# State scan of an S5 mixer on VectorE: products reordered, sums done in two halves

## The chip, the cores and the metric

One core of one Trainium2 chip. The metric is the device time of one execution of the whole program in microseconds (us); the median of the runs stands for a kernel. The engines are called PE (TensorE, the matrix engine), DVE (VectorE), ACT (ScalarE), POOL (GpSimd) and SP (SyncE, which issues transfers).

## The reference

An encoder of two layers over 1040 tokens (16 learned ones in front of 1024) of width 1024, all in float32. Layer 0 has a bidirectional S5 state-space mixer, layer 1 grouped-query attention, and each of them is followed by a SwiGLU channel mixer. What matters here is the recurrence of the S5 mixer, in both directions:

```
def _s5_combine(left, right):
    ...
    br = ar2 * br1 - ai2 * bi1 + br2
    bi = ar2 * bi1 + ai2 * br1 + bi2
...
    _, _, sr, si = lax.associative_scan(_s5_combine, (a_r, a_i, bu_r, bu_i), reverse=reverse, axis=1)
    return (jnp.einsum('blgp,gcp->blgc', sr, c_re) - jnp.einsum('blgp,gcp->blgc', si, c_im))
```

There are 64 groups of 16 channels, and each group has 64 complex states for each direction. A state is multiplied by a complex constant (abr, abi) and the input of the step is added to it.

## The kernel before

The S5 mixer takes 8 tokens as one step (T = 8), so that 1040 tokens make 130 steps (NK). Matrix products first form the inputs of all steps, then a scan carries the state from step to step, and then matrix products read the outputs from the states (L533). The scan is a loop over i from 2 to 129 in `s5_phase`, 128 steps one after the other, since each needs the state of the one before. Both directions lie on the partitions together: 64 partitions hold the states of the forward direction, 64 those of the backward one. On the free side a state has its real and its imaginary part for 64 groups, [2, 64], 128 elements.

One step is four instructions on DVE, L507 to L510:

```
V.tensor_tensor(out=TA, in0=SB[:, 0], in1=st, op=ALU.mult)
V.tensor_tensor(out=TB, in0=SB[:, 1], in1=st, op=ALU.mult)
V.tensor_tensor(out=TS, in0=TA, in1=bi, op=ALU.add)
V.tensor_tensor(out=nx, in0=TS, in1=TB[:, ::-1], op=ALU.add)
```

`st` and `nx` are the states of step i - 1 and i in the table XS (SBUF), which held the step's input in the same place before. `bi` is that input, copied ahead. The constants SB[:, 0] (real part, twice) and SB[:, 1] (imaginary part, once with its sign turned) and the product TB are three quarters of one PSUM tile, SBT, of 2 KB in each partition; the profile calls all three SB. TA and TS lie in SBUF. `TB[:, ::-1]` swaps real and imaginary part.

The order on each engine is that of the program text; nothing moves instructions. Semaphore waits are set by the framework from the tiles that instructions read and write, also between instructions of the same engine.

The loop also gives out other work by step number. `inputs` copies the inputs of four steps at a time to PSUM, on ACT, four steps ahead (L485, tile IN, two buffers). `e_batch` builds the matrices for the read-out on POOL (L379 to L383), and `inside` makes what the tokens of a step give to each other, with products on PE (L435, L457), copies on ACT and transfers. From the middle of the scan on, `swap` turns the order of the backward states, on ACT (L469, L472, L473); its last piece comes after the last step, and then the read-out starts (L533, 256 matrix products).

After the S5 mixer's core come its two linear layers, the channel mixer, attention, and the second channel mixer, which the change doesn't touch.

Of the kernel before, what the change touches and what calls it, by code (L numbers as in the profile page):

```python
# [13 lines left out]
ALU = mybir.AluOpType  # L14
# [5 lines left out]
G = 64  # L20
# [92 lines left out]
def s5_phase(nc, tc, P, a, ident, acc, xres, ydram, late):  # L113

    V, A, PE, PO = nc.vector, nc.scalar, nc.tensor, nc.gpsimd
# [256 lines left out]
    def e_batch(gb):  # L372

        gs = slice(NB * gb, NB * gb + NB)
        g0 = NB * gb % (G // 2)
        q_r, q_s, q_d = (bc(q[:, :, gs].rearrange("p s g -> p g s"), 3, CH) for q in E3)
        c_r, c_i, c_s = (bc(c[:, gs], 2, T) for c in (Cr, Ci, Cs))
        er, ei = (Eh[2 * gb // NG][:, i, g0:g0 + NB] for i in range(2))
        PO.tensor_tensor(out=ek, in0=c_s, in1=q_r, op=ALU.mult)  # L379
        PO.tensor_tensor(out=er, in0=c_i, in1=q_s, op=ALU.mult)  # L380
        PO.tensor_tensor(out=er, in0=ek, in1=er, op=ALU.subtract)
        PO.tensor_tensor(out=ei, in0=c_r, in1=q_d, op=ALU.mult)
        PO.tensor_tensor(out=ei, in0=ei, in1=ek, op=ALU.subtract)  # L383
# [27 lines left out]
    SB, TB = SBT[:, :2], SBT[:, 2]  # L411
# [8 lines left out]
    TA = rp.tile([128, 2, G], FP32, name="TA")  # L420
    TS = rp.tile([128, 2, G], FP32, name="TS")
# [42 lines left out]
    def swap(lo, hi):  # L464

        n = hi - lo
        t = psw.tile([128, 4, 2, G], FP32, tag="t", name="t")[64:, :n]
        m0, m1 = NK - hi, NK - lo
        A.copy(out=t, in_=XS[64:, lo:hi])  # L469
        yield  # L470
        for cs, cp in [(slice(0, 2), A.copy)] if lo else [(slice(0, 1), A.copy), (slice(1, 2), V.tensor_copy)]:
            cp(out=XS[64:, lo:hi, cs], in_=XS[64:, m1 - 1:m0 - 1 if m0 else None:-1, cs])  # L472
            cp(out=XS[64:, m0:m1, cs], in_=t[:, ::-1, cs])  # L473
# [3 lines left out]
    sw = [(lo, hi) for hi, lo in zip(cuts, cuts[1:])]  # L477
    begun = []
    IN = {}

    def inputs(i):

        n = min(4, NK - i)
        t = psc.tile([128, 4, 2, G], FP32, tag="in", name="IN", bufs=2)
        A.copy(out=t[:, :n], in_=XS[:, i:i + n])  # L485
        for k in range(n):
            IN[i + k] = t[:, k]

    inputs(2)
    for i in range(2, NK):  # L490
        for gb in range(NG):
            if i == 2 + int(E_PACE * gb):
                e_batch(gb)
            l0 = L_AT + int(L_PACE * gb)
            if i == l0:
                work[gb] = [inside(gb), l0]
        for gb in list(work):
            if i >= work[gb][1]:
                at = next(work[gb][0], None)
                if at is None:  # L500
                    del work[gb]
                else:
                    work[gb][1] = L_AT + int(L_PACE * gb) + at
        if i % 4 == 2 and i + 4 < NK:
            inputs(i + 4)
        st, nx, bi = XS[:, i - 1], XS[:, i], IN.pop(i)
        V.tensor_tensor(out=TA, in0=SB[:, 0], in1=st, op=ALU.mult)  # L507
        V.tensor_tensor(out=TB, in0=SB[:, 1], in1=st, op=ALU.mult)  # L508
        V.tensor_tensor(out=TS, in0=TA, in1=bi, op=ALU.add)  # L509
        V.tensor_tensor(out=nx, in0=TS, in1=TB[:, ::-1], op=ALU.add)  # L510
        if sw and not begun and i > NK // 2:
            begun.append((sw[0][0], swap(*sw.pop(0))))
            next(begun[-1][1])
        if begun and NK - 1 - begun[0][0] <= i - 1:
            next(begun.pop(0)[1], None)
# [11 lines left out]
    for ft in range(KT):  # L527
        for g0 in range(8 * ft, 8 * ft + 8, 2):
            b = bank()
            for j in range(2):  # L530
                g = g0 + j
                for c2 in range(2):
# [3 lines left out]
                            in1=b[:, :2 * NK].rearrange("p (g k) -> p g k", g=2), op=ALU.add)  # L536
# [694 lines left out]
def whole(nc, tc, a, out):  # L1231
# [45 lines left out]
    def late():  # L1277
# [3 lines left out]
        return w.split  # L1281

    s5_phase(nc, tc, P, a, ident, acc, xdram, ydram, late)
    con = P("const2")
    N.blk = con.tile([128, 128], FP32, name="blk")
# [303 lines left out]
```

## Time and profile before

| What | Value |
|---|---|
| Median of 3 runs | 2845.06 us (2843.23 to 2846.6) |
| The profiled execution's own time | 2844.93 us |
| Its span in the trace | 2843.2 us |
| PE busy | 2649.4 us, 93% |
| DVE busy | 1559.1 us, 55%, 3025 instructions |
| ACT busy | 1154.3 us, 41% |
| POOL busy | 515.3 us, 18% |
| Mean granted clock of PE | 0.967 of full speed |

The span goes from the first to the last instruction; the execution's own time has 1.7 us around it. The busy times overlap. A line such as L507 is the line of the kernel before; "out<-in" are tiles by the program's names.

### The profile page before, as it was taken

The numbers are of one execution on the slowest core, as the hardware profiler recorded it, in microseconds if no ns is written. First come the engines' busy times: TensorE is split into PE (matmuls) and PEld (weight loads), VectorE is DVE, ScalarE is ACT, GpSimd is POOL, SyncE is SP. The second block draws the span as 40 slices with busy tenths as digits, with TensorE's granted clock in tenths as the row PEclk, the third lists the DMA queues.
The fourth block names the chain that finished last, engine by engine and source line by source line (L and its number), as shares of the span: only waits on it lengthen the run. The fifth ranks groups of instructions, "written<-read, shape, count | busy, mean of one in ns | idle before, by whom it ended". The sixth has DMA issues, their size and how long they took to land.

```text
span 2843.2 us, 43155 instructions
## 1 busy us (share of the span) xinstructions
PE 2649.4 (93%) x17277; PEld 2546.5 (90%) x17277; DVE 1559.1 (55%) x3025; ACT 1154.3 (41%) x2138; POOL 515.3 (18%) x533
## 2 busy tenths in 40 slices
PE   7657899999999999989999998999999999999997
PEld 6446899999999999988988887888999999999996
DVE  9994545733333333358768888885563333333334
ACT  7463534322212212245557778774522222222225
POOL 0770332300000000043034434431310000000002
PEclk9778999999999999999999999999999999999998
DMA  6113652221111111112111111102111111111101
GB/s 150 24 38 102 230 175 72 77 80 45 47 51 45 45 52 45 45 45 87 48 24 39 27 24 49 28 19 98 45 38 46 52 45 45 45 45 45 45 31 60
DMA packets 124836, 167.41 MB, mean 59 GB/s; under 512 B 13499, under 2 KB 104971, under 8 KB 124635
## 3 DMA queue, kind: packets, MB, share of 16 engines
q1 hardware_dynamic: 118203, 141.22, 17.5%
q0 software_dynamic: 5712, 21.30, 2.2%
q8 instruction: 136, 2.23, 0.3%
q10 hardware_dynamic: 720, 2.13, 0.2%
q14 instruction: 65, 0.53, 0.1%
HBM read 126.41 MB, written 21.23 MB: 52 GB/s over the span
## 4 chain that ended last, share of the span: by engine, by line
PE 78%; DVE 13%; ACT 4%; issue 3%; DMA 2%; POOL 1%; SPq 0%; ACTq 0%; DVEq 0%; POOLq 0%
PE bk L694 22%; PE bk L695 22%; PE bk L696 22%; PE pv L1106 4%; PE pt L1084 3%; DVE mx L1064 3%; DVE pl L1097 2%; PE b L533 2%; ACT ph L1092 1%; DVE TA L507 1%; DVE SB L508 1%; DVE XS L510 1%; PE bx L347 1%; PE b L124 1%; DVE TS L509 1%
## 5 line engine op out<-in xcount | busy, mean ns | idle before, releaser
L694 PE MATMUL bk<-Hh,unit 128*128 128x348 f32 (+1 forms) x2928 | 956.4, 327 | 9.4 <-ACT Hh L784 5.8
L695 PE MATMUL bk<-Hl,unit 128*128 128x348 f32 (+1 forms) x2928 | 945.3, 323 | 1.1 <-DVE Hl L788 1.0
L696 PE MATMUL bk<-Hh,unit 128*128 128x348 f32 (+1 forms) x2928 | 943.8, 322 | 0.0
L694 PEld LDWEIGHTS bk<-Hh,unit 128*128 128x128 f32 x2928 | 555.2, 190 | 14.7 <-ACT Hh L784 5.4
L695 PEld LDWEIGHTS bk<-Hl,unit 128*128 128x128 f32 x2928 | 554.9, 190 | 6.4 <-DVE Hl L788 2.0
L696 PEld LDWEIGHTS bk<-Hh,unit 128*128 128x128 f32 x2928 | 554.7, 189 | 0.0
L858 DVE TENSOR_TENSOR sg<-sg,bk 128x348 f32<-128x348 f32 x132 | 68.1, 516 | 632.3 <-PE bk L696 624.5
L723 POOL TENSOR_TENSOR lns<-lns,lnsq 128x348 f32<-128x348 f32 (+1 forms) x72 | 70.0, 983 | 1550.5 <-ACT lnsq L721 1549.4
L694 PE MATMUL bk<-gt,unit 128*128 128x348 f32 (+1 forms) x1056 | 340.5, 322 | 0.0
L696 PE MATMUL bk<-gt,unit 128*128 128x348 f32 (+1 forms) x1056 | 339.1, 321 | 0.0
L695 PE MATMUL bk<-gt,unit 128*128 128x348 f32 (+1 forms) x1056 | 338.5, 321 | 0.0
L881 DVE TENSOR_TENSOR acc<-acc,bk 128x348 f32<-128x348 f32 (+1 forms) x480 | 237.5, 513 | 112.7 <-PE bk L696 112.7
L860 ACT CAST gt<-sg 128x348 fp32r<-128x348 f32 x132 | 63.7, 482 | 487.6 <-DVE sg L858 487.6
L1084 PE MATMUL pt<-ident,P 128*116 128x128 f32 (+1 forms) x1188 | 181.3, 279 | 44.1 <-DVE pl L1097 39.4
L1097 DVE TENSOR_TENSOR pl<-pt,ph 116x512 fp32r<-116x512 f32 (+3 forms) x340 | 204.4, 619 | 15.0 <-ACT ph L1092 13.4
L1084 PEld LDWEIGHTS pt<-ident,P 128*116 128x116 f32 (+1 forms) x1188 | 132.5, 136 | 80.4 <-issue 30.6
L1072 POOL TENSOR_SCALAR P<-P,l 128x1044 f32<-128x1044 f32 x132 | 149.8, 1146 | 291.0 <-PE pv L1106 174.4
L694 PEld LDWEIGHTS bk<-gt,unit 128*128 128x128 f32 x1056 | 199.0, 188 | 0.5 <-issue 0.2
L695 PEld LDWEIGHTS bk<-gt,unit 128*128 128x128 f32 x1056 | 198.9, 188 | 0.5 <-issue 0.2
L696 PEld LDWEIGHTS bk<-gt,unit 128*128 128x128 f32 x1056 | 198.7, 188 | 0.0
L1092 ACT CAST ph<-pt 116x512 fp32r<-116x512 f32 (+3 forms) x340 | 168.6, 535 | 73.9 <-PE pt L1084 59.7
L609 ACT CAST unit<-raw 128x1024 fp32r<-128x1024 f32 x110 | 113.2, 1046 | 209.7 <-DMA raw<-in_ffn_w_up_dram 173.1
(287 smaller groups left out, 3928.1 us busy)
## 6 DMA issues: line engine op xcount, KB each, us to landing
raw<-in_ffn_w_gate_dram SPq DMA_DIRECT2D x44, 512.0 KB
raw<-in_ffn_w_up_dram SPq DMA_DIRECT2D x44, 512.0 KB
raw<-in_ffn_w_down_dram SPq DMA_DIRECT2D x44, 512.0 KB
y<-xdram SPq DMA_DIRECT2D x16, 520.0 KB
QA<-QH SPq DMA_DIRECT2D x30, 260.0 KB
raw<-in_attn_w_qkv_dram SPq DMA_DIRECT2D x14, 512.0 KB
xdram<-acc SPq DMA_DIRECT2D x32, 130.0 KB
xres<-xn POOLq DMA_DIRECT2D x8, 520.0 KB, 5.1
```

Of the source, the lines that this page charges most:

```text
L609: A.copy(out=u[:, 0], in_=r)
L694: mm(out, wh, xh, start=(first and i == 0), stop=False)
L695: mm(out, wh, xl, start=False, stop=False)
L696: mm(out, wl, xh, start=False, stop=(last and i == n - 1))
L723: (nc.vector if on_dve else nc.gpsimd).tensor_tensor(out=part, in0=part, in1=sq, op=ALU.add)
L881: V.tensor_tensor(out=x, in0=x, in1=b, op=ALU.add)
L1064: V.tensor_reduce(out=k.mx, in_=k.S[:, :, :348], axis=mybir.AxisListType.XY, op=ALU.max, negate=True)
L1072: PO.tensor_scalar(out=k.P, in0=k.P, scalar1=k.l, scalar2=1.0, op0=ALU.mult, op1=ALU.mult)
L1084: PE.transpose(b[:m, w * i + 128 * x:w * i + 128 * x + 128], u.P[x][:, KB_N * kt:KB_N * kt + m], self.ident)
L1092: A.copy(out=u.ph[s][:m, :w], in_=u.t[s][:m, :w])
L1097: V.tensor_tensor(out=u.pl[s][:m, :w], in0=u.t[s][:m, :w], in1=u.ph[s][:m, :w].bitcast(FP32), op=ALU.subtract)
L1106: PE.matmul(u.o[:, :u.w], VAs[u.j][:m, kt], (u.ph, u.pl)[x][s][:m, c:c + u.w], start=(kt == 0 and x == 0), stop=(kt == KBS - 1 and x == 1))
```

## The change

In a step the product TB comes first, then TA. The sum TS and the sum nx are each done in two instructions, one for groups 0 to 31 and one for groups 32 to 63, so that a step has six instructions, and the 128 steps have 768 in place of 512. What is computed is the same, element by element. Lines behind L479 stand one lower in the changed kernel's text, those behind the step three lower; there TB is L508, TA L509, TS L511 and nx L513.

```diff
     IN = {}
+    halves = [slice(0, G // 2), slice(G // 2, G)]
...
         st, nx, bi = XS[:, i - 1], XS[:, i], IN.pop(i)
+        V.tensor_tensor(out=TB, in0=SB[:, 1], in1=st, op=ALU.mult)
         V.tensor_tensor(out=TA, in0=SB[:, 0], in1=st, op=ALU.mult)
-        V.tensor_tensor(out=TB, in0=SB[:, 1], in1=st, op=ALU.mult)
-        V.tensor_tensor(out=TS, in0=TA, in1=bi, op=ALU.add)
-        V.tensor_tensor(out=nx, in0=TS, in1=TB[:, ::-1], op=ALU.add)
+        for gs in halves:
+            V.tensor_tensor(out=TS[:, :, gs], in0=TA[:, :, gs], in1=bi[:, :, gs], op=ALU.add)
+        for gs in halves:
+            V.tensor_tensor(out=nx[:, :, gs], in0=TS[:, :, gs], in1=TB[:, ::-1, gs], op=ALU.add)
```

DVE before, in the scan, from the second product of one step to the first sum of the next, in which a new block of inputs begins. SB as an output is TB, SB as an input holds the constants or TB; behind each stand the semaphores that it waits for, DVE_49 for earlier instructions of DVE itself, Activation_49 for ACT:

```order
L508 TENSOR_TENSOR SB<-SB,XS 128x128 [waits DVE_49]
L509 TENSOR_TENSOR TS<-TA,IN 128x128
L510 TENSOR_TENSOR XS<-TS,SB 128x128 [waits DVE_49]
L507 TENSOR_TENSOR TA<-SB,XS 128x128 [waits DVE_49]
L508 TENSOR_TENSOR SB<-SB,XS 128x128 [waits DVE_49]
L509 TENSOR_TENSOR TS<-TA,IN 128x128 [waits Activation_49]
```

The first sum, L509, waits for no instruction of DVE; in one step of four it waits for the copy of the inputs.

DVE in the changed kernel, the same place, from the second product, now TA, to the sums of the next step:

```order
L509 TENSOR_TENSOR TA<-SB,XS 128x128 [waits DVE_49]
L511 TENSOR_TENSOR TS<-TA,IN 128x2x32 [waits DVE_49]
L511 TENSOR_TENSOR TS<-TA,IN 128x2x32
L513 TENSOR_TENSOR XS<-TS,SB 128x2x32 [waits DVE_49] x2
L508 TENSOR_TENSOR SB<-SB,XS 128x128 [waits DVE_49]
L509 TENSOR_TENSOR TA<-SB,XS 128x128 [waits DVE_49]
L511 TENSOR_TENSOR TS<-TA,IN 128x2x32 [waits DVE_49,Activation_49]
```

The first half of TS now follows TA directly and waits for DVE, in one step of four for ACT too; its second half waits for nothing, and each half of nx has a wait of its own.

## Rows read from the trace of the kernel before

**Rows 1.** The page, chain that ended last: shares by engine and by line.
```profile
PE 78%; DVE 13%; ACT 4%; issue 3%; DMA 2%; POOL 1%; SPq 0%; ACTq 0%; DVEq 0%; POOLq 0%
PE bk L694 22%; PE bk L695 22%; PE bk L696 22%; PE pv L1106 4%; PE pt L1084 3%; DVE mx L1064 3%; DVE pl L1097 2%; PE b L533 2%; ACT ph L1092 1%; DVE TA L507 1%; DVE SB L508 1%; DVE XS L510 1%; PE bx L347 1%; PE b L124 1%; DVE TS L509 1%
```

**Rows 2.** Busy time by stretch; last columns: granted clock, DMA share, GB/s.
```profile
84.00:234.00 150.00, 77.18 (x640) 55.75 (x640) 136.18 (x512) 77.10 (x165) 104.89 (x128) 0.68 0.16 36
...
225.00:234.00 9.00, 0.00 (x0) 0.00 (x0) 8.14 (x31) 3.70 (x9) 0.00 (x0) 0.50 0.00 0
234.00:238.00 4.00, 3.17 (x14) 3.17 (x15) 1.14 (x3) 2.74 (x4) 0.00 (x0) 0.50 0.00 2
```

**Rows 3.** The chain in order of time, 60 to 300 us: start, length, what.
```profile
86.93 0.30 DVE TA L507
...
233.98 0.41 ACT XS L472
234.41 0.38 ACT XS L473
234.83 57.21 PE b L533 x256
```

**Rows 4.** Timeline of DVE in the scan: start, length, instruction; first, third, last step.
```profile
84.59 0.29 DVE L507 TENSOR_TENSOR TA<-SB,XS 128x128 f32<-128x128 f32 x1 [1.33 <-ACT SB L414]
...
86.93 0.29 DVE L507 TENSOR_TENSOR TA<-SB,XS 128x128 f32<-128x128 f32 x1
87.25 0.30 DVE L508 TENSOR_TENSOR SB<-SB,XS 128x128 f32<-128x128 f32 x1
87.46 0.28 DVE L509 TENSOR_TENSOR TS<-TA,IN 128x128 f32<-128x128 f32 x1
87.77 0.29 DVE L510 TENSOR_TENSOR XS<-TS,SB 128x128 f32<-128x128 f32 x1
88.09 0.29 DVE L507 TENSOR_TENSOR TA<-SB,XS 128x128 f32<-128x128 f32 x1
...
232.76 0.29 DVE L507 TENSOR_TENSOR TA<-SB,XS 128x128 f32<-128x128 f32 x1
```

**Rows 5.** Groups by line, 84.5 to 234 us: busy us, mean ns | idle before.
```profile
L508 DVE TENSOR_TENSOR SB<-SB,XS 128x128 f32<-128x128 f32 x128 | 38.3, 299 | 4.4
L507 DVE TENSOR_TENSOR TA<-SB,XS 128x128 f32<-128x128 f32 x128 | 37.3, 291 | 5.7 <-ACT SB L414 1.3
L510 DVE TENSOR_TENSOR XS<-TS,SB 128x128 f32<-128x128 f32 x128 | 36.8, 288 | 4.4
L509 DVE TENSOR_TENSOR TS<-TA,IN 128x128 f32<-128x128 f32 x128 | 35.5, 277 | 0.0
```

**Rows 6.** Timeline of DVE, powers of the decay, 64 elements a partition.
```profile
16.19 0.23 DVE L105 TENSOR_TENSOR w<-PW 128x64 f32<-128x64 f32 x1
16.33 0.22 DVE L106 TENSOR_TENSOR w<-PW 128x64 f32<-128x64 f32 x1
16.58 0.23 DVE L107 TENSOR_TENSOR PW<-w,w 128x64 f32<-128x64 f32 x1
16.84 0.23 DVE L108 TENSOR_TENSOR w<-PW 128x64 f32<-128x64 f32 x1
16.98 0.22 DVE L109 TENSOR_TENSOR w<-PW 128x64 f32<-128x64 f32 x1
```

**Rows 7.** Timeline of DVE, two products of 512 elements a partition, one after the other.
```profile
75.31 0.68 DVE L105 TENSOR_TENSOR w<-PW,acT 128x512 f32<-128x512 f32 x1
75.91 0.68 DVE L106 TENSOR_TENSOR w<-PW,acT 128x512 f32<-128x512 f32 x1
```

**Rows 8.** Wait instructions on DVE's queue: ns min/median/max, first and last start, of lines L507, L535.
```profile
L507 DVEq EVENT_SEMAPHORE  x1: 21/21/21, 82.7 to 82.7; - x1
...
L535 DVEq EVENT_SEMAPHORE  x4: 49/50/50, 234.8 to 235.1; - x4
```

**Rows 9.** Groups by line on ACT, 84.5 to 234 us: the copies of the inputs.
```profile
L485 ACT COPY IN<-XS 128x512 f32<-128x512 f32 x32 | 18.8, 589 | 50.3 <-DVE TS L509 50.0
```

## Prediction

> **What bounds the kernel now.** I read the chain of waits first. By engine it is 78% PE and 13% DVE, and among its lines the four of the scan step, L507 to L510, have 1% each [rows 1]. So the scan is on the path although DVE as a whole isn't the bound. The table of stretches shows where: from 84 to 234 us DVE is busy for 136.18 of 150 us with 512 instructions, while PE has 77.18 us of work and stands at a granted clock of 0.68 [rows 2]. The chain in order of time then gives the ends of this stage: DVE step after step, two ACT copies at 233.98 and 234.41 us, and at 234.83 us the read-out of the states on PE, L533, which runs 57.21 us without a break [rows 3]. Nothing else holds L533 back, so whatever the scan loses or wins is passed on to it one for one.
>
> Inside the stage the reader should look at starts, not at busy time. The first step begins at 84.59 us and the last at 232.76 us [rows 4]; that is 127 steps in 148.17 us, 1166.7 ns each. Within one step TB starts 0.32 us after TA, TS only 0.21 us after TB, nx 0.31 us after TS, and the next TA 0.32 us after nx. The instructions take 291, 299, 277 and 288 ns [rows 5]. Three of the four therefore start some 35 ns after the one before has ended: these are hand-offs, the price of a wait on an instruction of the same engine. The fourth, TS, starts while TB still runs. I take 205 ns for that free slot: then 1166.7 - 205 - (291 + 277 + 288) leaves 105.7 ns, 35 ns for each of the three hand-offs; the rows have them as idle time, 4.4 us in front of 128 instructions [rows 5], 34 ns each.
>
> **Why TS is free.** TS reads TA, and TB had already waited for TA. That TB waits for TA is no matter of data: TB writes the third quarter of the PSUM tile SBT, TA reads the first. The wait goes by the tile. So before the change the one false wait lies between the products, and it pays for the true one, that of TS on TA.
>
> **The change, part by part.**
> The products change places. Now TA stands behind TB, reads the tile that TB has just written, and waits: the order of instructions shows a wait on DVE in its row. The cost of that pair is 299 + 35 = 334 ns, where before TA to TB cost 291 + 35 = 326 ns. But the sum TS now depends on the instruction right in front of it, TA, and its first half has a wait on DVE that it did not have: 291 + 35 = 326 ns, in the place of the free 205 ns. Nothing is left to run under TB.
>
> The sums become four instructions of 64 elements a partition in place of two of 128. A free slot of that size is in the trace, though in a two-dimensional form: the powers of the decay, where a product follows another without a wait after 0.14 us, twice [rows 6]. A free slot of 512 elements is 0.60 us [rows 7], so an element costs (600 - 205) / 384 = 1.03 ns, and 64 elements fewer than 128 give 205 - 66 = 139 ns. I take 139. The first half of TS to the second: free, 139. The second half of TS to the first of nx: the latter waits for the first half of TS, which ends 277 - 66 = 211 ns after its start and with 35 ns of hand-off lets go at 246 ns. The free slot is up at 2 x 139 = 278 ns, later, so the wait costs nothing; should the margin of 32 ns be gone, it would cost what exceeds it. The first half of nx to the second: free by the same count, 139. The last half to the next step's TB: TB reads the whole state, so it waits, 288 - 66 + 35 = 257 ns. Together 3 x 139 + 257 = 674 ns, where TS and nx with their hand-offs cost 277 + 288 + 70 = 635 ns before. Halving hides two hand-offs less well than it adds two slots: it is worth +39 ns by itself.
>
> The new step is 334 + 326 + 674 = 1334 ns, 167 ns more than 1166.7. Times 128 steps: 21.4 us.
>
> In each fourth step the first half of TS waits for two semaphores, DVE and ACT, since a new block of inputs comes in; such a double wait leaves an instruction of its own on the queue, and the trace has them at 21 ns and at 50 ns [rows 8]. 32 of them at 35 ns are 1.1 us; the ends are 0 (it passes while TA runs) and 32 x 50 = 1.6 us.
>
> Other engines gain time. ACT's copies of the inputs wait 50.0 us in all for TS [rows 9]; they run four steps ahead, so a later TS delays nothing that DVE waits for (idle in front of L509 is 0.0 [rows 5]). If that cover went, a copy of 0.59 us would show in front of TS 32 times, 19 us. The work on PE, POOL and ACT that the loop sets out by step number is spread over a longer stage and stays under it. The clock doesn't enter: it is at the lower level, 0.50 (1.2 GHz), in the last 9 us of the scan and in the first 4 us of the read-out [rows 2], PE being idle before; a longer scan leaves it there.
>
> Sum: 21.4 + 1.1 = 22.5 us, all of it on the path. The profiled execution took 2844.93 us (span 2843.2), 0.13 us under the median of the runs, 2845.06, so no correction is due: 2844.93 + 22.5 = 2867.4, told as **2867 us**, +0.8%. A difference of under 0.2%, 5.7 us, can't be told from none.
>
> **The bounds.** The form of the halves, two runs of 32, is not in the trace. From above: slots of 145 ns (0.14 is rounded to 10 ns), hand-offs of 45 ns and 50 ns for the double wait give 344 + 336 + 3 x 145 + 267 = 1382 ns and 1.6 us, +29 us. From below: if a half took its free slot by its elements alone, 66 ns, the waits would decide: nx's first half starts 246 ns after that of TS, its second 312 ns, the next TB 569 ns; the step is 334 + 326 + 569 = 1229 ns, +8 us. I take the middle value since the rows of 64 elements give 0.14 directly, and let the range run from 2858 to 2875.
>
> **The rivals.**
> (a) TA does not wait for TB, since the two quarters of SBT don't overlap. Then TB to TA is 205 in place of 334 ns, 129 x 128 = 16.5 us less: 2851 us, just at the edge of what can be told. For it: the data. Against: before, with the same two quarters, TB starts only after TA has ended [rows 4], and the wait stands in TA's row.
> (b) The halves of nx wait for all of TS. Then nx's first half starts at 139 + 246 = 385 ns rather than 278, 107 ns more, 13.7 us in all: 2881 us. For it: waits here can go by whole tiles. Against: both halves of nx have a wait in the order; if the first waited for the second half of TS, nothing would be left for the other to wait for, as TS has none behind TB now.
> (c) No instruction starts before the one in front has ended. The step is then the sum of durations, 299 + 291 + 2 x 211 + 2 x 222 = 1456 ns, 289 ns more, 37 us: 2882 us. Against: TS starts 205 ns into TB's 299 [rows 4, 5]. The Trainium skill, page "VectorE: DVE Perf Modes", section "The DRAIN you can't avoid", says that the next operation doesn't start until the pipe is empty, and its rules advise to keep the number of operations low; but a sentence there lets one that isn't held start earlier. The trace sides with that sentence.
> (d) Faster: TA is free as in (a), and the halves take 66 ns slots as in the lower bound. The step is 205 + 326 + 569 = 1100 ns, 67 ns less: 2844.93 - 8.5 = 2836 us. It decides once TA is free and a slot is under 126 ns, from 205 + 326 + 3 s + 257 = 1167. For it: the PSUM product's latency is then covered by TA. Against: the two rows of 0.14, and the wait on TA.
>
> **How the numbers follow.** My forecast 0.88; (a) 0.03; (b) 0.04; (c) 0.01; (d) 0.02; 0.02 for what lies between (a) and 2858. The range of the forecast alone holds 0.88, more than 8 in 10, and (a) to (d) may stay outside. Slower by over 0.2%: 0.88 + 0.04 + 0.01, half of (a) and the last 0.02, 0.95 rounded; within 0.2%: 0.03; faster: 0.02.
>
> **What would show it.** Right: steps 1.33 us apart; TA starts after TB's end, the first half of TS after TA's end; 256 halves of about 211 ns at L511 and 256 of about 222 ns at L513; slots of 0.14 us between them; the read-out starting some 22 us later and nothing after it changed in length. Wrong: TA starting within TB's 0.30 us (a, d), nx's first half starting after the end of TS's second (b), slots as long as the halves (c), or a read-out that starts later while the span doesn't grow.

## The result, and the profile after

The changed kernel took 2868.16 us (median of 4 runs, 2866.67 to 2869.57), the one before 2845.51 us beside it (4 runs, 2843.23 to 2846.6): a ratio of 1.0076, with a 95% interval of 1.0061 to 1.0091. The forecast was 2867 us. It is slower by 22.65 us, where the sum said 22.5.

The timeline of DVE in the scan of the changed kernel; columns as in [rows 4]. Where two halves follow each other, the view merges them into one row, with the time from the start of the first to the end of the second:

```profile
83.74 0.30 DVE L508 TENSOR_TENSOR SB<-SB,XS 128x128 f32<-128x128 f32 x1 [1.09 <-ACT SB L414]
84.07 0.29 DVE L509 TENSOR_TENSOR TA<-SB,XS 128x128 f32<-128x128 f32 x1
84.47 0.35 DVE L511 TENSOR_TENSOR TS<-TA,IN 128x64 f32<-128x64 f32 x2
84.74 0.35 DVE L513 TENSOR_TENSOR XS<-TS,SB 128x64 f32<-128x64 f32 x2
85.12 0.30 DVE L508 TENSOR_TENSOR SB<-SB,XS 128x128 f32<-128x128 f32 x1
85.45 0.29 DVE L509 TENSOR_TENSOR TA<-SB,XS 128x128 f32<-128x128 f32 x1
85.78 0.35 DVE L511 TENSOR_TENSOR TS<-TA,IN 128x64 f32<-128x64 f32 x2
86.04 0.35 DVE L513 TENSOR_TENSOR XS<-TS,SB 128x64 f32<-128x64 f32 x2
86.42 0.30 DVE L508 TENSOR_TENSOR SB<-SB,XS 128x128 f32<-128x128 f32 x1
...
252.32 0.30 DVE L508 TENSOR_TENSOR SB<-SB,XS 128x128 f32<-128x128 f32 x1
```

Three things are to be seen. First, TA starts 0.33 us after TB, when TB has ended, and the first half of TS 0.33 us after TA: no instruction runs under another between the products, where before TS ran under TB. Second, from the first half of TS to the next step's TB it is 0.64 us, about the 0.63 us that the whole sums took in [rows 4] (87.46 to 88.09 us). Third, the first step shown is one in which new inputs begin, and in it TS starts 0.40 us after TA; it takes 1.38 us where the next takes 1.30. The mean over the scan is (252.32 - 83.74) / 127 = 1327 ns, 161 ns over the 1167 of before, 20.6 us in 128 steps.

The groups of the changed kernel by line, 84.5 to 256 us, which answer to [rows 5] and [rows 9]:

```profile
L511 DVE TENSOR_TENSOR TS<-TA,IN 128x64 f32<-128x64 f32 x256 | 45.2, 217 | 6.6
L513 DVE TENSOR_TENSOR XS<-TS,SB 128x64 f32<-128x64 f32 x256 | 44.3, 215 | 0.1
...
L486 ACT COPY IN<-XS 128x512 f32<-128x512 f32 x31 | 18.3, 589 | 60.9 <-DVE TS L511 60.6
```

The idle time went from the whole second sum, 4.4 us before, to the first half of the first one, 6.6 us; in front of nx 0.1 us is left. ACT's copies wait longer than before, 60.6 us, and no idle time of DVE is put down to them.

The wait instructions of L511 on DVE's queue, with the columns of [rows 8]:

```profile
L511 DVEq EVENT_SEMAPHORE  x32: 21/21/21, 84.4 to 249.0; - x32
```

The chain of the changed kernel in order of time, at the end of the scan, beside [rows 3], and the stretch in which the read-out starts, beside [rows 2]:

```profile
254.11 0.38 ACT XS L473
254.53 57.27 PE b L536 x256
```

```profile
254.00:258.00 4.00, 3.47 (x15) 3.47 (x16) 0.86 (x3) 2.44 (x4) 0.00 (x0) 0.50 0.00 0
```

The read-out starts at 254.53 us, 19.70 us later; as this scan began 0.85 us earlier, its length from the first product to the read-out grew by 20.55 us, from 150.24 to 170.79 us. The read-out itself is as long as before (57.27 us against 57.21), and the clock at its start is again 0.50.

### The profile page after: what moved, and what is told of

Read it like the earlier page. It is cut to its first block, busy times and chain, and to the rows that moved or that the text cites. A ratio compares the mean times of both kernels' runs of the same rounds, so it can differ in the third digit from the quotient of the medians.

```text
span 2864.9 us, 43443 instructions
## 1 busy us (share of the span) xinstructions
PE 2656.1 (93%) x17277; PEld 2550.6 (89%) x17277; DVE 1575.7 (55%) x3281; ACT 1154.6 (40%) x2138; POOL 515.7 (18%) x533
## 4 chain that ended last, share of the span: by engine, by line
PE 76%; DVE 14%; ACT 4%; issue 3%; DMA 1%; POOL 1%; SPq 0%; ACTq 0%; DVEq 0%; POOLq 0%
PE bk L698 21%; PE bk L697 21%; PE bk L699 21%; PE pv L1109 4%; PE pt L1087 3%; DVE mx L1067 3%; DVE pl L1100 2%; PE b L536 2%; ACT ph L1095 1%; DVE TS L511 1%; DVE SB L508 1%; DVE TA L509 1%; DVE XS L513 1%; DVE acc L753 1%; ACT P L1071 1%
```

## The experiments

The quantity to compare, beside the time, is the stretch from the first product of the scan to the first matrix product of the read-out: 150.24 us before, 170.79 us after the change. It leaves out what varies in other stages. The ratios are against runs of the kernel before taken beside each group: 2847.17 us at the median for the first four kernels here, 2846.78 us for the other four.

### The order alone, the halves alone

The order alone, against the kernel before:

```diff
+        V.tensor_tensor(out=TB, in0=SB[:, 1], in1=st, op=ALU.mult)
         V.tensor_tensor(out=TA, in0=SB[:, 0], in1=st, op=ALU.mult)
-        V.tensor_tensor(out=TB, in0=SB[:, 1], in1=st, op=ALU.mult)
```

The halves alone, against the changed kernel:

```diff
-        V.tensor_tensor(out=TB, in0=SB[:, 1], in1=st, op=ALU.mult)
         V.tensor_tensor(out=TA, in0=SB[:, 0], in1=st, op=ALU.mult)
+        V.tensor_tensor(out=TB, in0=SB[:, 1], in1=st, op=ALU.mult)
```

Expected of the order alone: 

> The products in the changed order (TB, then TA), both sums whole. Theory, that the false wait of TA on TB puts the true wait of TS on TA into the open: TB to TA 334, TA to TS 326, TS to nx 312, nx to TB 321 ns, a step of about 1295 ns, 128 ns over before; with the double wait in 32 steps (70 ns each as the changed kernel shows it) 18 to 19 us, about 2864 us. Rival, that the two extra instructions cost the time: about as before, 2846 us.

Measured: 2865.34 us, ratio 1.0067 (1.0054 to 1.0080). Expected of the halves alone: 

> The sums in halves, the products in the old order (TA, then TB). Theory: the first half of TS is free behind TB (205 ns), the four halves take about 645 ns from the first to the next step, a step of 326 + 205 + 645 = 1176 ns, +1 us: 2846 to 2848 us. Rival, that halving costs the time: 2862 us or more.

Measured: 2848.01 us, ratio 1.0003 (0.9994 to 1.0011). The stretch from scan to read-out is 169.61 us with the order alone (84.28 to 253.89 us) and 150.81 us with the halves alone (85.99 to 236.80 us): of the change's 20.55 us the order makes 19.4, the halves by themselves 0.6. Both times lie within 1.4 us of what was expected. The timeline of DVE, first the order alone, then the halves alone:

```profile
121.19 0.30 DVE L507 TENSOR_TENSOR SB<-SB,XS 128x128 f32<-128x128 f32 x1
121.52 0.29 DVE L508 TENSOR_TENSOR TA<-SB,XS 128x128 f32<-128x128 f32 x1
121.91 0.29 DVE L509 TENSOR_TENSOR TS<-TA,IN 128x128 f32<-128x128 f32 x1
122.23 0.29 DVE L510 TENSOR_TENSOR XS<-TS,SB 128x128 f32<-128x128 f32 x1
122.56 0.30 DVE L507 TENSOR_TENSOR SB<-SB,XS 128x128 f32<-128x128 f32 x1
```

```profile
121.12 0.29 DVE L508 TENSOR_TENSOR TA<-SB,XS 128x128 f32<-128x128 f32 x1
121.45 0.30 DVE L509 TENSOR_TENSOR SB<-SB,XS 128x128 f32<-128x128 f32 x1
121.66 0.34 DVE L511 TENSOR_TENSOR TS<-TA,IN 128x64 f32<-128x64 f32 x2
121.91 0.35 DVE L513 TENSOR_TENSOR XS<-TS,SB 128x64 f32<-128x64 f32 x2
122.29 0.29 DVE L508 TENSOR_TENSOR TA<-SB,XS 128x128 f32<-128x128 f32 x1
```

In the first the sums stand whole and every instruction waits for the one in front (0.33, 0.39, 0.32, 0.33 us; the 0.39 is a step with a double wait). In the second TS starts 0.21 us after TB as before, and the step is 1.17 us. That the two added instructions cost the time is refuted; on top of the changed order they make 1.2 us (169.61 to 170.79).

### Is the wait between the products one by the tile?

The constants that TA reads move to a tile of their own. In the first pair of kernels that tile is in SBUF; the edit is made once to the changed kernel, once to the kernel before:

```diff
-    A.copy(out=SB[:, 0], in_=bc(PW[:, 0, 8], 1, 2))
+    SA = tab.tile([128, 2, G], FP32, name="SA")
+    A.copy(out=SA, in_=bc(PW[:, 0, 8], 1, 2))
...
-        V.tensor_tensor(out=TA, in0=SB[:, 0], in1=st, op=ALU.mult)
+        V.tensor_tensor(out=TA, in0=SA, in1=st, op=ALU.mult)
```

Expected with the changed order: 

> The changed kernel, with the constants that TA reads in a tile of their own in SBUF, so that TA shares no tile with TB. Theory, that the wait of TA on TB goes by the shared PSUM tile: TB to TA falls from 334 to about 205 ns, the rest stays, a step of 205 + 326 + 645 = 1176 ns (and up to 70 ns in 32 steps): 2846 to 2849 us. Rival, that an instruction behind one that writes PSUM must wait for its end: TB to TA stays at 334 ns and the time at 2868 us.

Expected with the old order: 

> The kernel before, with the constants that TA reads in a tile of their own. Theory: TB follows TA after 205 ns, TS follows TB after 205 ns (its wait on TA, 326 ns, is over by then), the sums keep 312 + 321 ns: a step of about 1043 ns, 124 ns less, -16 us: about 2829 us. Rival, that TB must run behind TA's end for another reason than the tile: as before, 2845 us.

Measured: 2875.88 us, ratio 1.0100 (1.0086 to 1.0114), and 2873.16 us, ratio 1.0090 (1.0076 to 1.0104). Both forecasts of the time failed, and yet, where POOL is idle, the waits are what the theory said. The timeline of DVE with the old order and the tile in SBUF, and after it that of POOL in the same kernel:

```profile
120.60 0.29 DVE L508 TENSOR_TENSOR TA<-SA,XS 128x128 f32<-128x128 f32 x1
120.81 0.29 DVE L509 TENSOR_TENSOR SB<-SB,XS 128x128 f32<-128x128 f32 x1
121.01 0.28 DVE L510 TENSOR_TENSOR TS<-TA,IN 128x128 f32<-128x128 f32 x1
121.32 0.29 DVE L511 TENSOR_TENSOR XS<-TS,SB 128x128 f32<-128x128 f32 x1
121.64 0.29 DVE L508 TENSOR_TENSOR TA<-SA,XS 128x128 f32<-128x128 f32 x1
...
122.68 2.05 DVE L508 TENSOR_TENSOR TA<-SA,XS 128x128 f32<-128x128 f32 x1
124.66 0.29 DVE L509 TENSOR_TENSOR SB<-SB,XS 128x128 f32<-128x128 f32 x1
```

```profile
116.35 1.26 POOL L383 TENSOR_TENSOR E<-E,ek 128x512 f32<-128x512 f32 x1
121.13 0.31 POOL L445 TENSOR_TENSOR dI<-dI,f 16x64 f32<-16x64 f32 x1 [3.52 <-ACT f L442]
...
122.43 1.09 POOL L379 TENSOR_TENSOR ek<-Cs,E 128x512 f32<-128x512 f32 x1
123.49 1.09 POOL L380 TENSOR_TENSOR E<-cT,E 128x512 f32<-128x512 f32 x1
```

From 117.6 to 121.1 us POOL is idle, and there TB follows TA after 0.21 us and the step takes 1.04 us, as worked out. When POOL starts on its 512-element products at 122.43 us, the next TA, begun at 122.68 us, lasts 2.05 us in place of 0.29, until 0.15 us after POOL's second product is done; TB and the sums keep their lengths. TA is the one instruction in this kernel's step that now takes both operands from SBUF.

Was it POOL, and both operands in SBUF? The next three kernels give TA's constants a tile of their own, or spare the need of one, with an operand in PSUM for every instruction:

A PSUM tile of their own, once in the changed kernel and once in the kernel before, with three banks for the rest in place of four:

```diff
-    P.close("s5_psx")
+    P.close("s5_psx", "s5_ps")
+    ps = P("s5_ps", bufs=3, space=PSUM)
...
-    A.copy(out=SB[:, 0], in_=bc(PW[:, 0, 8], 1, 2))
+    SA = psc.tile([128, 4, 2, G], FP32, name="SA")[:, 0]
+    A.copy(out=SA, in_=bc(PW[:, 0, 8], 1, 2))
...
-        V.tensor_tensor(out=TA, in0=SB[:, 0], in1=st, op=ALU.mult)
+        V.tensor_tensor(out=TA, in0=SA, in1=st, op=ALU.mult)
```

No write to the tile of the constants, in the kernel before:

```diff
-    SB, TB = SBT[:, :2], SBT[:, 2]
+    SB = SBT[:, :2]
...
-    TS = rp.tile([128, 2, G], FP32, name="TS")
+    TB = rp.tile([128, 2, G], FP32, name="TB")
...
-        V.tensor_tensor(out=TS, in0=TA, in1=bi, op=ALU.add)
-        V.tensor_tensor(out=nx, in0=TS, in1=TB[:, ::-1], op=ALU.add)
+        V.tensor_tensor(out=bi, in0=TA, in1=bi, op=ALU.add)
+        V.tensor_tensor(out=nx, in0=bi, in1=TB[:, ::-1], op=ALU.add)
```

Expected of the changed order with its own PSUM tile: 

> The changed kernel with the constants of TA in a PSUM tile of their own (the pool of banks for the other work goes from four to three from here on). Theory: as meant for the run with that tile in SBUF, without POOL in it: TB to TA 205, TA to the first half of TS 326, the halves 645 ns, a step of 1176 ns, 70 ns more in 32 steps, +3 us: 2848 to 2851 us, if three banks do for the rest. Rival, that POOL is not what lengthened TA there: TA of 500 ns on the mean again, 2870 us or more.

Expected of the old order with it: 

> The kernel before with the constants of TA in a PSUM tile of their own (three banks for the rest). Theory: a step of 1043 ns throughout, 16 us less: 2830 to 2832 us. Rival as in the run before: 2870 us or more.

Expected without a write to the tile of the constants: 

> The kernel before with its order and whole sums, but nothing written to the tile of the constants: TB goes to SBUF and TS is written over the input in its PSUM tile, so each of the four instructions still reads one operand from PSUM and one from SBUF. Theory of two conditions (no false wait by a shared PSUM tile; no instruction with both operands in SBUF, which stands still while POOL works): TA to TB 205, TB to TS 205, TS to nx and nx to TA 312 to 335 ns, a step of 1043 to 1065 ns over the whole scan, with POOL busy or idle, 13 to 16 us less: 2831 to 2834 us. Rival, that a free TB behind TA meets POOL in any case: TA or TB of up to 2.4 us again and 2865 us or more.

Measured, in this order: 2851.39 us, ratio 1.0015 (1.0006 to 1.0024); 2833.34 us, ratio 0.9950 (0.9938 to 0.9963); 2830.97 us, ratio 0.9950 (0.9937 to 0.9962). The first lies 0.4 us and the second 1.3 us over its forecast, the third at the lower end of its own. The groups of DVE by line, 88 to 210 us, with the constants in their own PSUM tile and the old order:

```profile
L509 DVE TENSOR_TENSOR TA<-SA,XS 128x128 f32<-128x128 f32 x117 | 34.1, 291 | 4.1
L510 DVE TENSOR_TENSOR SB<-SB,XS 128x128 f32<-128x128 f32 x117 | 33.8, 289 | 0.0
L512 DVE TENSOR_TENSOR XS<-TS,SB 128x128 f32<-128x128 f32 x116 | 33.2, 286 | 4.0
L511 DVE TENSOR_TENSOR TS<-TA,IN 128x128 f32<-128x128 f32 x116 | 32.1, 277 | 0.9 <-ACT IN L487 0.8
```

TA is back at 291 ns with POOL at work, and of the three hand-offs of before one is gone: no idle time stands in front of TB. The timeline of DVE in the kernel that writes nothing to the tile of the constants, while POOL works (it has L381 from 120.75 us on and L382 from 121.98):

```profile
121.70 0.29 DVE L507 TENSOR_TENSOR TA<-SB,XS 128x128 f32<-128x128 f32 x1
121.91 0.28 DVE L508 TENSOR_TENSOR TB<-SB,XS 128x128 f32<-128x128 f32 x1
122.11 0.28 DVE L509 TENSOR_TENSOR IN<-TA,IN 128x128 f32<-128x128 f32 x1
122.43 0.29 DVE L510 TENSOR_TENSOR XS<-IN,TB 128x128 f32<-128x128 f32 x1
122.75 0.29 DVE L507 TENSOR_TENSOR TA<-SB,XS 128x128 f32<-128x128 f32 x1
```

A step is 1.05 us, and the stretch from scan to read-out 135.43 us (86.94 to 222.37). With the constants in their own PSUM tile it is 135.49 us in the old order (84.36 to 219.85), and 153.23 us with the changed order and the halves (85.04 to 238.27). The timeline of DVE in the latter:

```profile
120.74 0.30 DVE L510 TENSOR_TENSOR SB<-SB,XS 128x128 f32<-128x128 f32 x1
120.95 0.28 DVE L511 TENSOR_TENSOR TA<-SA,XS 128x128 f32<-128x128 f32 x1
121.26 0.35 DVE L513 TENSOR_TENSOR TS<-TA,IN 128x64 f32<-128x64 f32 x2
...
121.91 0.30 DVE L510 TENSOR_TENSOR SB<-SB,XS 128x128 f32<-128x128 f32 x1
```

TA now follows TB after 0.21 us, and a step takes 1.17 us. So without the false wait the change costs 17.7 us, nearly the 20.55 that it costs with it. The two costs are separate: the false wait costs 0.12 to 0.13 us a step in either order (1.17 against 1.04 us, 1.30 against 1.17), and what the order costs is the true wait, since TS stands right behind TA. The runs do not tell whether two smaller tiles within the same 2 KB of PSUM would do: here the operands were parted by a whole tile of 2 KB, or by one in SBUF.

### Halves that are used

Seven instructions, against the kernel of the old order with its own PSUM tile:

```diff
+        for gs in halves:
+            V.tensor_tensor(out=TA[:, :, gs], in0=SA[:, :, gs], in1=st[:, :, gs], op=ALU.mult)
-        V.tensor_tensor(out=TA, in0=SA, in1=st, op=ALU.mult)
         V.tensor_tensor(out=TB, in0=SB[:, 1], in1=st, op=ALU.mult)
...
+        for gs in halves:
+            V.tensor_tensor(out=TS[:, :, gs], in0=TA[:, :, gs], in1=bi[:, :, gs], op=ALU.add)
+        for gs in halves:
+            V.tensor_tensor(out=nx[:, :, gs], in0=TS[:, :, gs], in1=TB[:, ::-1, gs], op=ALU.add)
```

Expected: 

> Constants of TA in a PSUM tile of their own, and seven instructions: TA in two halves, TB whole, TS in two halves, nx in two halves. Theory: with no false wait every true wait is met by the slots between (six of 133 and one of 205 ns), a step of about 1005 to 1015 ns, 19 to 21 us less: 2826 to 2829 us; the halves pay only here, where what waits for a half can go on. Rival, that seven slots cost more than the hand-offs they hide: 2832 us or more.

Measured: 2831.95 us, ratio 0.9949 (0.9937 to 0.9962), outside what was expected and no faster than the two before. The timeline of DVE in it:

```profile
120.53 0.34 DVE L511 TENSOR_TENSOR TA<-SA,XS 128x64 f32<-128x64 f32 x2
120.79 0.28 DVE L512 TENSOR_TENSOR SB<-SB,XS 128x128 f32<-128x128 f32 x1
120.99 0.33 DVE L514 TENSOR_TENSOR TS<-TA,IN 128x64 f32<-128x64 f32 x2
121.25 0.33 DVE L516 TENSOR_TENSOR XS<-TS,SB 128x64 f32<-128x64 f32 x2
121.51 0.34 DVE L511 TENSOR_TENSOR TA<-SA,XS 128x64 f32<-128x64 f32 x2
```

The step did fall, to 0.98 us, the shortest of all. But the stretch is 134.55 us (84.60 to 219.15), where 128 such steps are 125.4. The waits of DVE in the scan, and the shares of the chain between 84 and 219 us, say why for the most part:

```profile
DVE TS L514 <- ACT IN L488: 6.4, 7, 1.5
```

```profile
by line: SPq L453 28.4%; DMA M<-Z 17.4%; issue 10.8%; DVE XS L516 4.5%; DVE TS L514 4.4%; DVE TA L511 3.9%; POOL E L381 3.8%; POOL E L383 3.8%; DVE SB L512 3.5%; POOL dI L446 3.2%; POOL E L380 3.2%; POOL E L382 3.2%; POOL Z L447 3.1%; POOL 
```

DVE now waits seven times, 6.4 us in all, for ACT's copies of the inputs (0.8 us with four instructions, in the groups above, and nothing in the kernel before), and SP's issues of the transfers of `inside` (L453, 28.4%) lead the chain. It looks as if the work that the loop gives out by step number has become the bound. That was read from the chain, not tested by a change of those transfers.

## Why the prediction was right

**What bounds the kernel** held: the scan's length went through to the read-out one for one, and the read-out did not change. Of the 22.65 us between the medians 20.55 lie in the scan; the span grew by 21.7 us, and as the changed kernel's read-out starts only 19.70 us later, about 2 us of the profiled execution came after it began and are not explained by the scan. The runs of the kernel before differ by more among themselves (2843.23 to 2846.6 us).

**The products** came out as worked: 0.33 us from TB to TA, 0.33 us from TA to TS, where 334 and 326 ns stood. The order alone costs 19.4 us, nearly the whole; TS after TA, 0.33 us in place of the 0.21 after TB, makes about 15 us of it in 128 steps.

**Why TS was free** was half right. TS did wait for nothing, but the false wait did not pay for that. In the kernel with the tile split and the old order, TB starts 0.21 us after TA and TS 0.20 us after TB (120.60, 120.81, 121.01 us), 0.41 us after TA, when TA has ended without any wait between the products. What covers the true wait is that TB stands between TA and TS. The false wait bought nothing and cost 0.12 us a step, before the change and after it. The sum was not touched by this, since it priced each pair from its own rows.

**The halves** were too dear: 674 ns expected, 0.64 us measured, since the two slots from the first half of TS to the first of nx take 0.27 us (84.47 to 84.74) rather than 278 ns, and the first half of nx to the next step 0.38 us (84.74 to 85.12) rather than 139 + 257 = 396 ns. The term of +39 ns by itself is +5 ns in the run with the halves alone (0.6 us in 128 steps). The first half of nx indeed waits for nothing: 0.1 us idle in 256.

**The double wait** was too cheap: TS starts 0.40 us after TA in those steps and 0.33 in the others, 70 ns rather than 35, 2.2 us in 32 steps rather than 1.1. Of its own instruction only 21 ns show.

**The time** was met in part by luck. The errors of these two terms partly cancel in the scan, 22.5 us forecast and 20.55 measured, and the 2 us after the start of the read-out, which nobody forecast, fill up the rest. The lower bound as worked, +8 us, is 2853 us; the range began at 2858 without a reason given.

**The rivals.** (a) fell: TA waits for TB, and only when it shares no tile with TB do 0.21 us part them (120.74 to 120.95 us). (b) fell with the 0.27 us above: in TS, a tile in SBUF, the wait went by the half. (c) fell, since two halves of 215 ns take 0.35 us together, so that they start 0.13 to 0.14 us apart. The page "VectorE: DVE Perf Modes" of the Trainium skill, section "The DRAIN you can't avoid", was right here in its sentence on instructions that aren't held, not in its rule that each next one waits for an empty pipe. (d) had its first condition met only when the tile was split, and its second nowhere.

## What to carry to other kernels

In a chain of short instructions on one engine, count the waits that stand between neighbours, true and false ones, before counting instructions. Where an instruction needs the result of another, look for a third to put between them. Here that third covered the true wait; putting the pair the other way round took the cover away and cost about 15 us. The false wait covered nothing: without it the same four instructions took 1.04 to 1.05 us a step in place of 1.17. Where one instruction writes a PSUM tile and its neighbour reads another part of it, the tile should be split, but not by moving an operand to SBUF beside another one while POOL is busy. Halving shortened a step (from 1.04 to 0.98 us) only where what waits for a half was free to go on at once, and even there the whole did not get faster.

## What the runs showed of the hardware

An instruction of DVE with both operands in SBUF stood still while POOL worked: TA took 279 ns at the least and 2437 ns at the most in the run with the changed order, with a mean of 518 ns up to 240 us. With that operand in a PSUM tile of its own it took 278 to 283 ns throughout. The Trainium skill, page "SBUF — State Buffer", section "SBUF: two separate sides", has it as an exclusive lock on a shared pair of ports, held for a whole instruction, between a POOL instruction that reads SBUF and a DVE instruction with two SBUF inputs. The runs agree, with one thing more: the TA of 2.05 us above began under POOL's first product and was not let in when that one ended at 123.52 us, but only after the second. The trace of before showed it already, outside the scan: two rows of its timelines, of DVE and of POOL,

```profile
18.88 2.33 DVE L110 TENSOR_TENSOR PW<-w,w 128x128 f32<-128x128 f32 x1
```

```profile
18.64 2.41 POOL L281 TENSOR_TENSOR Hs<-bT 128x1024 f32<-128x1024 f32 x1 [16.95 <-ACT bT L204]
```

where a sum of 128 elements with both operands in SBUF lasts 2.33 us, until a POOL instruction that began before it is done.
